# A two-layer encoder on one core: the MLP in two phases through DRAM, with the up product as a chained seven-product block product

## The chip, the core and the metric

The kernel runs on one core of a Trainium2 chip. The metric is the device time of one launch in microseconds. The kernel before takes 1725.45 us (median of three runs, 1725.27 to 1726.40).

## The reference, cut to what matters

Two sequences of 512 and 256 tokens (768 together) with 1024 features pass through two layers of different mixers. Behind each mixer stands the same MLP with 4096 hidden features:

```python
def trunk(x, w):
    for layer in range(DEPTH):                 # two layers
        ...                                    # mix: Hyena and attention, or conformer and pooling
        x = layer_norm(DN_ALPHA * x + mix, w['ln1_g'][layer], w['ln1_b'][layer])
        h = jnp.square(jax.nn.relu(x @ w['mlp_w1'][layer])) @ w['mlp_w2'][layer]
        x = layer_norm(DN_ALPHA * x + h, w['ln2_g'][layer], w['ln2_b'][layer])
    return x
```

All is float32. The kernel gets float32 precision out of TensorE's rounded format (fp32r) by splitting every operand into a high part (a ScalarE copy that rounds) and a low part (a VectorE subtraction of the high part from the source). A product of two split operands is three matmuls, high by high, high by low and low by high.

## The kernel before

The MLP is the function `mlp`, called once per layer. `self.acc[0..5]` holds six token tiles of 128 tokens by 1024 features; `x` holds the same, transposed and split, in `quad` tiles. The 32 tiles of 128 hidden features are taken in eight chunks of four.

**Up.** `feature_tile` makes one hidden tile for 384 tokens: eight contraction steps of three matmuls with 384 columns. A hidden tile needs two such calls, so one layer has 32 x 2 x 8 x 3 = 1536 matmuls of 384 columns. The weights of a tile come by `weights` (load `raw`, copy `wh`, subtraction `wl`). ScalarE applies ReLU (L507) and square (L509) and the tile stays in SBUF as `sq`.

**Down.** The second product of the first seven chunks is a two by two block product in Winograd's form: tokens, hidden tiles and output columns are cut in halves, and seven block products take the place of eight. `operands` makes the left operands of a pair of hidden tiles (four sums of 384 columns on VectorE, L518, then splits). `moving` loads four blocks of weights (`mraw`), makes four sums of them on GpSimd (L518) and splits the seven right operands. A block product is three PSUM banks (`s`, `b`, `o`) by two hidden tiles by three matmuls of 512 columns: 18. Each product is added to the token tiles or to partial sums `u` by VectorE (L569, L594), or from `u` by GpSimd (L569). The last chunk is a plain product, so that the token tiles end one after another and each goes through its layer norm.

**Order.** A generator hands out two products behind each hidden tile, so up and down alternate on TensorE all through the MLP. Loads and weight splits are given high priority and run ahead. Five weight slots in two rings (`self.rings`) hold the split `wh` and `wl`. Each engine works its own instructions in order; SyncE (SP) issues the loads in order, and each load waits there until its buffer is free.

## Time and profile before

| | us |
|---|---|
| median of three runs | 1725.45 |
| span of the profiled execution | 1726.3 |
| TensorE (PE) busy | 1635.3 |
| VectorE (DVE) busy | 1310.8 |
| ScalarE (ACT) busy | 741.0 |
| GpSimd (POOL) busy | 676.7 |

The first MLP lies at about 468 to 945 us of the span, the second at 1212 to 1711 us. The profile lists busy time, waits by releaser, instructions in order of time, and in windows the busy time of every engine with the clock that TensorE was granted (1.00 is its full 2.4 GHz). PE rows show an instruction from its start to its modelled end, and successive matmuls overlap, so their pace is read from start to start.

### The profile page before, as it was taken

What the parts mean: (1) busy time and instruction counts of PE and PEld (TensorE: products, weight loads), DVE (VectorE), ACT (ScalarE), POOL (GpSimd) and SP (SyncE); (2) the same over time, 40 slices, a digit from 0 to 9 for tenths busy, and PEclk for the clock granted to TensorE, in tenths of its full rate; (3) what the DMA queues carried; (4) which work ended last, traced back from release to release, by engine and by line L of the source; (5) the groups of instructions that cost most, each with busy time, mean ns of one, the idle gap of its engine ahead of it and who ended that gap; (6) DMA issues with size and microseconds to landing.
All of it is one profiled execution on the core that took longest, in us unless ns stands there. A gap on an engine that the chain in (4) does not pass through costs nothing.

```text
span 1726.3 us, 21545 instructions
## 1 busy us (share of the span) xinstructions
PE 1635.3 (95%) x8308; PEld 1444.5 (84%) x8308; DVE 1310.8 (76%) x1828; ACT 741.0 (43%) x1115; POOL 676.7 (39%) x423
## 2 busy tenths in 40 slices
PE   8999979999899999999999899687999999999997
PEld 6878767878799999999998788466999999999996
DVE  5786887874777677777776899998677777777767
ACT  5633335662344344344342455445444434434431
POOL 1364552110624325324421489754422532442323
PEclk9999979999999999999999899898999999999999
DMA  6331142023211221221111212122222122112101
GB/s 233 115 110 63 37 141 75 28 96 122 98 61 50 86 69 42 86 86 49 62 62 62 66 52 93 43 74 68 93 84 74 41 82 86 50 62 86 61 26 73
DMA packets 43366, 131.32 MB, mean 76 GB/s; under 512 B 5040, under 2 KB 7544, under 8 KB 43264
## 3 DMA queue, kind: packets, MB, share of 16 engines
q1 hardware_dynamic: 43264, 129.95, 22.8%
q8 instruction: 65, 1.06, 0.3%
q14 instruction: 37, 0.30, 0.1%
HBM read 122.03 MB, written 7.90 MB: 75 GB/s over the span
## 4 chain that ended last, share of the span: by engine, by line
PE 74%; DVE 18%; ACT 3%; issue 2%; DMA 2%; POOL 1%; SPq 0%; DVEq 0%; ACTq 0%; POOLq 0%
PE a L275 11%; PE a L274 11%; PE a L276 11%; PE b L274 5%; PE b L275 5%; PE o L275 4%; PE b L276 4%; PE o L276 4%; PE o L274 4%; PE s L275 4%; PE s L274 4%; PE s L276 4%; DVE co L1276 3%; DVE wl L249 2%; DVE o L1276 2%
## 5 line engine op out<-in xcount | busy, mean ns | idle before, releaser
L274 PE MATMUL a<-quad,wh 128*128 128x384 f32 (+2 forms) x1248 | 411.3, 330 | 2.5 <-ACT quad L241 1.3
L275 PE MATMUL a<-quad,wh 128*128 128x384 f32 (+2 forms) x1248 | 411.7, 330 | 0.4 <-DVE quad L249 0.2
L276 PE MATMUL a<-quad,wl 128*128 128x384 f32 (+2 forms) x1248 | 411.4, 330 | 0.0
L518 POOL TENSOR_TENSOR mraw<-mraw,mraw 128x1024 f32<-128x1024 f32 x56 | 175.3, 3140 | 245.5 <-issue 233.6
L569 POOL TENSOR_TENSOR acc<-acc,u 128x512 f32<-128x512 f32 x84 | 130.7, 1588 | 328.0 <-DVE u L594 328.0
L249 DVE TENSOR_TENSOR wl<-mraw,wh 128x1024 fp32r<-128x1024 f32 x98 | 135.1, 1378 | 143.6 <-ACT wh L241 143.6
L274 PEld LDWEIGHTS a<-quad,wh 128*128 128x128 f32 x1248 | 235.0, 188 | 7.9 <-ACT quad L241 1.8
L275 PEld LDWEIGHTS a<-quad,wh 128*128 128x128 f32 x1248 | 235.3, 189 | 6.2 <-DVE quad L249 1.4
L249 DVE TENSOR_TENSOR wl<-raw,wh 128x1024 fp32r<-128x1024 f32 x112 | 150.0, 1339 | 117.3 <-ACT wh L241 117.1
L276 PEld LDWEIGHTS a<-quad,wl 128*128 128x128 f32 x1248 | 235.4, 189 | 1.5
L241 ACT ACTIVATE wh<-raw 128x1024 fp32r<-128x1024 f32 x127 | 134.0, 1056 | 177.8 <-PE a L275 79.9
L241 ACT ACTIVATE wh<-mraw 128x1024 fp32r<-128x1024 f32 x98 | 104.0, 1061 | 172.5 <-PE a L275 100.9
L507 ACT ACTIVATE sq<-a 128x384 f32<-128x384 f32 x128 | 61.4, 480 | 146.2 <-PE a L276 133.3
L274 PE MATMUL s<-quad,wh 128*128 128x512 f32 (+1 forms) x224 | 87.0, 388 | 10.9 <-ACT quad L241 6.0
L1273 POOL TENSOR_TENSOR c<-c,c 128x512 f32<-128x512 f32 (+1 forms) x63 | 77.0, 1224 | 43.6 <-ACT c L1272 40.3
L569 DVE TENSOR_TENSOR acc<-acc,s 128x512 f32<-128x512 f32 x112 | 73.9, 680 | 24.9 <-ACT u L603 24.9
L569 DVE TENSOR_TENSOR acc<-acc,o 128x512 f32<-128x512 f32 x124 | 82.8, 678 | 9.9 <-PE o L276 9.7
L275 PE MATMUL s<-quad,wh 128*128 128x512 f32 (+1 forms) x224 | 87.0, 388 | 1.4 <-DVE quad L249 1.4
L276 PE MATMUL s<-quad,wl 128*128 128x512 f32 (+1 forms) x224 | 86.5, 386 | 0.0
L569 DVE TENSOR_TENSOR acc<-acc,b 128x512 f32<-128x512 f32 x124 | 82.0, 679 | 1.2 <-PE b L276 1.0
L249 POOL TENSOR_TENSOR wl<-raw,wh 128x1024 fp32r<-128x1024 f32 x15 | 39.2, 2612 | 70.6 <-ACT wh L241 59.5
L1276 DVE SCALAR_TENSOR_TENSOR co<-hp,cols,co 128x256 f32<-128x256 f32 x88 | 66.0, 792 | 0.1
(516 smaller groups left out, 3865.5 us busy)
## 6 DMA issues: line engine op xcount, KB each, us to landing
raw<-in_w SPq DMA_DIRECT2D x72, 512.0 KB
mraw<-in_w SPq DMA_DIRECT2D x56, 512.0 KB
raw<-in_w_hy SPq DMA_DIRECT2D x12, 512.0 KB
raw<-in_w_oi SPq DMA_DIRECT2D x12, 512.0 KB
raw<-in_w_oo SPq DMA_DIRECT2D x12, 512.0 KB
raw<-in_w_eo SPq DMA_DIRECT2D x8, 512.0 KB
raw<-in_w_mla SPq DMA_DIRECT2D x6, 512.0 KB
zy<-in_xT SPq DMA_DIRECT2D x12, 256.0 KB
```

The source lines that it names most:

```text
L241: self.nc.scalar.activation(dst, src, AF.Copy)
L249: e.tensor_tensor(out=dst, in0=src, in1=hi.bitcast(F32), op=ALU.subtract)
L274: mm(out, a[0], b[0], start=start, stop=False)
L275: mm(out, a[0], b[1], start=False, stop=False)
L276: mm(out, a[1], b[0], start=False, stop=stop)
L507: nc.scalar.activation(sq[m][:, off : off + n], ps[:, :n], AF.Relu)
L518: eng.tensor_tensor(out=o, in0=a, in1=b, op=op)
L569: (nc.vector if eng == "dve" else nc.gpsimd).tensor_tensor(out=av, in0=av, in1=v, op=ALU.add)
L1273: nc.gpsimd.tensor_tensor(out=c2, in0=c2, in1=c3, op=ALU.add)
L1276: last = nc.vector.scalar_tensor_tensor(out=v, in0=hp[:, k : k + n], scalar=w(k), in1=v, op0=ALU.mult, op1=ALU.add)
```

## The change

`mlp` is split into `up_phase` and `down_phase`, and the hidden operands go through DRAM between them.

- **Up phase.** Hidden tiles are taken in 16 pairs. The first two pairs are plain, as before (4 x 2 x 8 x 3 = 192 matmuls of 384 columns). For the other 14 the up product is itself a two by two block product (features, hidden tiles and tokens by halves): seven products of 4 x 3 matmuls of 384 columns, 84 for a pair. The three accumulators `c`, `y`, `z` are each one PSUM bank; a later product is chained on an earlier one by accumulating in the same bank, and a copy (`u1`, `u2`, `v7`) is taken in between.
- **Operands of the up phase.** `token_operands` makes four sums of `acc` for each of three token tile pairs, 128 x 512 each (three on GpSimd, nine on VectorE), transposes them (48 transposes of 128 x 128) and splits them. `operands(q)` loads two weight tiles, makes four 512-column sums on GpSimd and cuts 3.5 tiles into high and low parts; before, a pair needed two.
- **Store.** The squares and their sums for the down product (four sums of 384 columns on VectorE per pair, as before) go unsplit to DRAM: `a`, `b`, `s` and `s4`, 1.376 MB for a pair. The last two pairs are stored plain.
- **Down phase.** The 14 pairs come in chunks of 4, 4, 4 and 2 pairs. Each of the seven products reloads its left operand (`hr`, up to 128 x 1536) and splits it (`hh`, `hl`), and is three banks by n pairs by three matmuls of 512 columns. Products are chained in PSUM here too, so a chunk of four pairs needs 15 additions of 512 columns on VectorE and six on GpSimd. Eight sums of 1024 columns on GpSimd make the weights of a chunk (two for each of the four). The last two pairs follow as a plain product with the layer norms.
- The residual factor on `acc` stands between the phases (six GpSimd instructions). The pool of the next layer's `x` is opened after the down phase.

The diff, cut to its core:

```diff
+    def token_operands(self, xt, tmp):
+        for t in range(3):
+            a, b = self.acc[t], self.acc[t + 3]
...
+            for i, p, q, e in (
+                (0, b[:, :512], a[:, :512], nc.vector), (2, b[:, 512:], b[:, :512], nc.gpsimd),
+                (1, b[:, 512:], d[0], nc.vector), (3, a[:, 512:], d[1], nc.vector),
+            ):
+                e.tensor_tensor(out=d[i], in0=p, in1=q, op=sub)
+            for i in (1, 2, 0, 3):
...
+                    nc.tensor.transpose(ps[:, j * P : j * P + P], d[i][:, j * P : j * P + P], self.ident)
+                self.split(*(q[:, :, t * P : t * P + P] for q in T_[i]), src)
...
+            def operands(q):
...
+                    wa = self.cut(ra)
+                    tt(s[:, h0], rb[:, h0], rb[:, h1], add)
+                    tt(s[:, h1], s[:, h0], ra[:, h0], sub)
+                    ws = self.cut(s)
+                    tt(rb[:, h0], ra[:, h0], rb[:, h0], sub)
+                    wb = self.cut(rb)
+                    tt(ra[:, h1], ra[:, h1], s[:, h1], sub)
+                    w4 = self.cut(ra[:, h1], 512)
...
+                product("1", c, True)
+                nc.scalar.activation(u1, c, AF.Copy)
+                product("2", y, True)
+                tt(ha[:, :HT], u1, y, add, nc.vector)
+                product("6", c, False)
+                nc.scalar.activation(u2, c, AF.Copy)
+                product("7", z, True)
+                nc.scalar.activation(v7, z, AF.Copy)
+                product("5", c, False)
+                tt(hb[:, HT:], v7, c, add, nc.vector)
+                product("4", z, False)
+                tt(hb[:, :HT], u2, z, add, nc.vector)
+                product("3", c, False)
...
+                store(q, ha, hb)
...
+            def left(q0, n, i, c):
...
+                    r = self.t(db, [P, 4, HT], "hr", bufs=3)[:, :n]
+                    nc.sync.dma_start(r, src if c is None else src[:, :, c * HT : c * HT + HT])
+                    v = [self.t(db, [P, 4, HT], f"h{g}", F32R, bufs=3)[:, :n] for g in "hl"]
+                    self.split(*v, r)
...
+            for q0, n in CHUNKS:
...
+                product(xb, 0, 0, True)
+                copies(u)
+                out(0, 0, u, nc.gpsimd)
+                product(yb, 1, 0, True)
+                out(0, 0, yb)
+                product(xb, 2, 1, False)
+                copies(u2)
+                out(1, 0, u2, nc.gpsimd)
+                product(yb, 0, 1, True)
+                out(1, 1, yb)
+                product(xb, 2, 0, False)
+                out(1, 1, xb)
+                product(yb, 1, 1, False)
+                out(1, 0, yb)
+                product(xb, 3, None, False)
+                out(0, 1, xb)
...
+        self.up_phase(l, x, hs)
+        xs.close()
+        for t in range(NT):
+            nc.gpsimd.tensor_scalar(out=self.acc[t], in0=self.acc[t], scalar1=ALPHA, scalar2=None, op0=ALU.mult)
+        self.down_phase(l, hs)
```

Where this moves instructions is read from the built programs. First SP, in the middle of the MLP before: loads of both weights follow one another (`in_w1_0` and `in_w2_0` are the weights of the first layer).

```order
L540 DMA mraw_1153_6109<-in_w2_0 128x1024 [waits DMAHW5_49,Pool_49]
L540 DMA mraw_1154_6111<-in_w2_0 128x1024 [waits DMAHW6_49,DVE_49]
L266 DMA raw_1193_6329<-in_w1_0 128x1024 [waits DVE_49]
L540 DMA mraw_1155_6113<-in_w2_0 128x1024 [waits DMAHW0_49,DVE_49]
L540 DMA mraw_1156_6115<-in_w2_0 128x1024 [waits DMAHW1_49,DVE_49]
```

On SP in the kernel after, at the end of the up phase; `hs` and `hp` are the hidden operands in DRAM, `a` and `b` are squares written by ScalarE:

```order
L555 DMA hp1_864_4236<-b_1185_6297 128x768 [waits Activation_49]
L555 DMA hp0_863_4235<-a_1184_6296 128x768 [waits Activation_49]
L555 DMA hp1_866_4238<-b_1204_6427 128x768 [waits DMAHW5_49,DVE_49,Activation_49]
L555 DMA hp0_865_4237<-a_1203_6426 128x768 [waits DMAHW6_49,Activation_49]
L687 DMA hr_1223_6555<-hs0_847_4219 128x4x384 [waits DMAHW7_49,PE_49]
L654 DMA mraw_1226_6561<-in_w2_0 128x1024 [waits DMAHW0_49]
L687 DMA hr_1238_6627<-hs1_848_4220 128x4x384 [waits DMAHW1_49,PE_49]
L654 DMA mraw_1227_6563<-in_w2_0 128x1024 [waits DMAHW2_49,PE_49]
L687 DMA hr_1245_6682<-hs2_849_4221 128x4x384 [waits DMAHW3_49]
L654 DMA mraw_1228_6565<-in_w2_0 128x1024 [waits DMAHW4_49]
```

The first load of the down phase stands behind the store of the last pair; the loads of `in_w2_0` that stood among the loads of `in_w1_0` now all come after it.

Second GpSimd, at a chunk's start. Before, the four weight sums of a chunk stood in one piece ahead of the additions to `acc`:

```order
L518 TENSOR_TENSOR mraw_898_4573<-mraw_899_4575,mraw_898_4573 128x1024 [waits DMAHW1_49,DMAHW0_49,DVE_49]
L518 TENSOR_TENSOR mraw_899_4575<-mraw_900_4577,mraw_899_4575 128x1024 [waits DMAHW2_49,Pool_49]
L518 TENSOR_TENSOR mraw_907_4613<-mraw_900_4577,mraw_898_4573 128x1024
L518 TENSOR_TENSOR mraw_901_4579<-mraw_901_4579,mraw_907_4613 128x1024 [waits DMAHW3_49,DVE_49,Pool_49]
L569 TENSOR_TENSOR acc3_778_3647<-acc3_778_3647,u0_895_4564 128x512 [waits DVE_49]
```

And GpSimd after, at the start of the first chunk of the down phase (`mraw_1248` and `mraw_1249` are the right operand of the third product):

```order
L640 TENSOR_TENSOR mraw_1226_6561<-mraw_1230_6569,mraw_1226_6561 128x1024 [waits DMAHW0_49,DMAHW6_49,DVE_49,Pool_49]
L694 TENSOR_TENSOR acc0_775_3644<-acc0_775_3644,u0_1217_6549 128x512 [waits Activation_49]
L640 TENSOR_TENSOR mraw_1227_6563<-mraw_1231_6571,mraw_1227_6563 128x1024 [waits DMAHW2_49,DMAHW7_49,DVE_49,PE_49]
L694 TENSOR_TENSOR acc1_776_3645<-acc1_776_3645,u1_1218_6550 128x512 [waits Activation_49]
L694 TENSOR_TENSOR acc2_777_3646<-acc2_777_3646,u2_1219_6551 128x512 [waits Activation_49]
L640 TENSOR_TENSOR mraw_1248_6688<-mraw_1232_6573,mraw_1226_6561 128x1024 [waits DMAHW0_49,PE_49,Pool_49]
L640 TENSOR_TENSOR mraw_1230_6569<-mraw_1232_6573,mraw_1230_6569 128x1024
L640 TENSOR_TENSOR mraw_1249_6689<-mraw_1233_6575,mraw_1227_6563 128x1024 [waits DMAHW1_49,Pool_49]
L640 TENSOR_TENSOR mraw_1231_6571<-mraw_1233_6575,mraw_1231_6571 128x1024
```

The sum that the third product needs now stands behind the additions to `acc`, which wait for ScalarE's copies of the first product.

Third ScalarE. Before, the copies of summed weights stood among ReLU, squares and hidden operands:

```order
L241 ACTIVATE wh_1072_5605<-mraw_1068_5597 128x1024 [waits DMAHW5_49,PE_49]
L241 ACTIVATE obh_1009_5233<-sq_1001_5167 128x768 [waits PE_49]
L507 ACTIVATE sq_1042_5431<-a_1043_5432 128x384 [waits DVE_49,PE_49]
L241 ACTIVATE wh_1078_5639<-mraw_1077_5637 128x1024 [waits Pool_49]
L241 ACTIVATE wh_1084_5675<-raw_1083_5673 128x1024 [waits DMAHW3_49,PE_49]
```

After, at the start of the down phase, behind the first splits:

```order
L251 ACTIVATE wh_1243_6639<-mraw_1229_6567 128x1024 [waits DMAHW5_49]
L719 ACTIVATE u0_1217_6549<-s_1211_6543 128x512 [waits PE_49]
L719 ACTIVATE u1_1218_6550<-b_1212_6544 128x512 [waits PE_49]
L719 ACTIVATE u2_1219_6551<-o_1213_6545 128x512 [waits PE_49]
L251 ACTIVATE hh_1255_6744<-hr_1254_6742 128x1536 [waits DMAHW2_49,DVE_49]
L251 ACTIVATE hh_1262_6799<-hr_1261_6797 128x1536 [waits DMAHW3_49,DVE_49,PE_49]
L251 ACTIVATE wh_1250_6692<-mraw_1248_6688 128x1024 [waits Pool_49]
L251 ACTIVATE wh_1252_6696<-mraw_1249_6689 128x1024 [waits Pool_49]
```

The copy `hh_1262`, the left operand of the fifth product, waits for PE (its buffer is that of the second product) and stands ahead of `wh_1250`, which the third product needs.

## Rows read from the trace of the kernel before

**Rows 1.** The page: the span, and busy time of each engine.

```profile
span 1726.3 us, 21545 instructions
...
PE 1635.3 (95%) x8308; PEld 1444.5 (84%) x8308; DVE 1310.8 (76%) x1828; ACT 741.0 (43%) x1115; POOL 676.7 (39%) x423
```

**Rows 2.** Windows: busy us of each engine, granted clock, DMA share, GB/s.

```profile
core 0: us, PE busy (x) PEld busy (x) DVE busy (x) ACT busy (x) POOL busy (x), PEclk, DMA share, GB/s
...
448.00:456.00 8.00, 3.93 (x19) 3.00 (x17) 8.00 (x13) 4.58 (x7) 6.54 (x4) 0.71 0.64 194
460.00:500.00 40.00, 38.26 (x222) 37.14 (x221) 24.65 (x28) 17.20 (x26) 16.02 (x7) 1.00 0.17 62
500.00:560.00 60.00, 60.00 (x309) 55.08 (x309) 45.99 (x58) 26.32 (x36) 17.31 (x9) 1.00 0.22 71
700.00:760.00 60.00, 60.00 (x308) 54.93 (x307) 43.57 (x54) 25.69 (x34) 22.12 (x10) 1.00 0.19 62
```

**Rows 3.** Waits of PE in 470 to 940 us, all of them.

```profile
PE a L274 <- ACT sq L507: 1.2, 1, 1.2
```

**Rows 4.** PE in order of time: start, duration, instruction.

```profile
699.71 0.33 PE L274 MATMUL a<-quad,wh 128*128 128x384 f32 x1
...
704.91 0.39 PE L274 MATMUL s<-wh,obh 128*128 128x512 f32 x1
...
710.84 0.39 PE L276 MATMUL b<-wh,oal 128*128 128x512 f32 x1
```

**Rows 5.** PE in order of time: transposes in the layer norm ahead of the MLP.

```profile
447.42 0.60 PE L410 MATMUL o<-ident,acc 128*128 128x128 f32 x4
447.86 0.60 PE L410 MATMUL b<-ident,acc 128*128 128x128 f32 x4
```

**Rows 6.** Instructions by line, 470 to 940 us: count, busy us, mean ns, idle before.

```profile
L249 DVE TENSOR_TENSOR wl<-mraw,wh 128x1024 fp32r<-128x1024 f32 x49 | 67.7, 1382 | 70.3 <-ACT wh L241 70.3
L569 DVE TENSOR_TENSOR acc<-acc,o 128x512 f32<-128x512 f32 x58 | 38.7, 678 | 5.0 <-PE o L276 4.9
L241 ACT ACTIVATE wh<-raw 128x1024 fp32r<-128x1024 f32 x32 | 33.9, 1059 | 47.5 <-PE a L275 29.5 <-PE o L276 15.4 <-DMA raw<-in_w_oi 2.7
L518 POOL TENSOR_TENSOR mraw<-mraw,mraw 128x1024 f32<-128x1024 f32 x28 | 87.7, 3143 | 121.6 <-issue 116.4 <-DVE wl L249 4.7
L569 POOL TENSOR_TENSOR acc<-acc,u 128x512 f32<-128x512 f32 x42 | 65.4, 1589 | 162.7 <-DVE u L594 162.7
L598 POOL TENSOR_SCALAR acc<-acc 128x1024 f32<-128x1024 f32 x1 | 2.8, 2772 | 0.0
```

**Rows 7.** POOL and DVE in order of time, working together at 476 us.

```profile
475.76 7.74 POOL L518 TENSOR_TENSOR mraw<-mraw,mraw 128x1024 f32<-128x1024 f32 x3 [4.67 <-DVE wl L249]
...
478.62 2.63 DVE L518 TENSOR_TENSOR s<-s,sq 128x384 f32<-128x384 f32 x1
```

**Rows 8.** DVE in order of time at 706 us, where POOL has nothing to do.

```profile
706.08 1.23 DVE L249 TENSOR_TENSOR wl<-mraw,wh 128x1024 fp32r<-128x1024 f32 x1 [3.92 <-ACT wh L241]
707.23 0.68 DVE L569 TENSOR_TENSOR acc<-acc,s 128x512 f32<-128x512 f32 x1
707.82 0.55 DVE L518 TENSOR_TENSOR s<-sq,sq 128x384 f32<-128x384 f32 x1
708.29 0.68 DVE L569 TENSOR_TENSOR acc<-acc,b 128x512 f32<-128x512 f32 x1
```

**Rows 9.** Line L518 by form: count, shortest, median and longest ns, first and last start.

```profile
L518 POOL TENSOR_TENSOR mraw<-mraw,mraw x28: 2399/2712/4817, 475.8 to 871.2; 128x1024 f32<-128x1024 f32 x28
```

**Rows 10.** DMA 456.8 to 466.2 us in 40 slices, and SP's five issues there.

```profile
GB/s 0 0 0 0 157 157 192 331 418 349 401 314 401 418 349 453 366 349 279 314 296 366 384 366 418 436 401 436 401 453 366 471 366 279 174 105 87 52 52 0
...
456.88 0.33 SPq L266 DMA_DIRECT2D raw<-in_w  x1
457.26 1.91 SPq L540 DMA_DIRECT2D mraw<-in_w  x4
```

**Rows 11.** The chain of waits in order of time, a load that was waited for.

```profile
413.09 6.80 DMA raw<-in_w
```

More of the change, by code (lines that the diff above doesn't have):

```diff
@@ L202, in _layout, with __init__ @@
     return {k: np.ascontiguousarray(v) for k, v in out.items()}
+class _Slot(list):
+    def __init__(self, parts, chunk):
+        super().__init__(parts)
+        self.chunk = chunk
 class _Encoder:
@@ L270, in weights, with mm3, mm @@
         return h, l
-    def mm3(self, out, a, b, start, stop):
-        mm = self.nc.tensor.matmul
+    def mm3(self, out, a, b, start, stop, more=False):
+        def mm(*k, **kw):
+            self.nc.tensor.matmul(*k, skip_group_check=more, **kw)
         mm(out, a[0], b[0], start=start, stop=False)
@@ new lines, in down_phase, with tt, raw_tile, moving @@
+    def down_phase(self, l, hs):
+        nc, w2 = self.nc, self.d[f"w2_{l}"]
+        add, sub = ALU.add, ALU.subtract
+        def tt(o, a, b, op, eng=nc.gpsimd):
+            eng.tensor_tensor(out=o, in0=a, in1=b, op=op)
+        with self.pool("db") as db:
+            def raw_tile():
+                return self.t(db, [P, 1024], "mraw", bufs=12)
+            def moving(gs):
+                def load(h, c):
+                    r = []
+                    for g in gs:
+                        with self.tc.high_priority():
+                            v = raw_tile()
+                            nc.sync.dma_start(v, w2[g, h, c])
+                        r.append(v)
+                    return r
+                def cut(vs):
@@ L564, in moving @@
                 yield cut(b21)
                 yield cut(b22)
[L567 to L577 removed]
+            def left(q0, n, i, c):
+                with self.tc.high_priority():
+                    r = self.t(db, [P, 4, HT], "hr", bufs=3)[:, :n]
+                    src = hs[q0].chunk[i]
+                    nc.sync.dma_start(r, src if c is None else src[:, :, c * HT : c * HT + HT])
+                    v = [self.t(db, [P, 4, HT], f"h{g}", F32R, bufs=3)[:, :n] for g in "hl"]
+                    self.split(*v, r)
+                return v
@@ new lines, in into, with product @@
+            def into(t, c, v, eng):
+                av = self.acc[t][:, c * 512 : c * 512 + 512]
+                eng.tensor_tensor(out=av, in0=av, in1=v, op=add)
+            for q0, n in CHUNKS:
+                w = moving(range(q0 // 2, (q0 + n) // 2))
+                xb, yb = ([self.bank2(g) for g in "sbo"] for _ in range(2))
+                u = [self.t(db, [P, 512], f"u{j}", bufs=2) for j in range(3)]
+                u2 = [self.t(db, [P, 512], f"u{j}", bufs=2) for j in range(3)]
+                def product(pss, i, c, start):
+                    a, b = left(q0, n, i, c), next(w)
@@ L631, in mlp @@
-            ops = []
-            for i in (0, 2):
-                ops.append(operands(*up(tiles[0][i : i + 2])))
-            for e in range(NE - 1):
-                down = products(e, ops)
-                ops, hid = [], {}
-                for i, m in enumerate(tiles[e + 1]):
-                    (sq,) = up((m,))
-                    if e == NE - 2:
-                        hid[m] = [q for q in zip(*halves("oa" if i < 2 else "ob", sq))]
-                    elif i % 2:
-                        ops.append(operands(prev, sq))
-                    prev = sq
-                    next(down)
@@ L645, in mlp, with copies @@
-            if xp:
-                xq = self.quads(xp)
-            else:
-                xq = None
-            rows = [raw_tile() for _ in range(2)]
-            for j, v in enumerate(rows):
-                nc.sync.dma_start(v, self.d["rows"][row + j : row + j + 1, :].to_broadcast([P, D]))
-            e = NE - 1
-            ws = [[self.weights(w2[c, 2 * e + j]) for j in range(2)] for c in range(2)]
+                        into(3 * r + j, c, v, eng)
+                def copies(us):
+                    for v, ps in zip(us, xb):
+                        nc.scalar.activation(v, ps, AF.Copy)
```

277 lines of the change are left out of this document (148 added, 129 removed).

## The prediction

> **What bounds the kernel now.** I read the windows first. In the middle of an MLP TensorE is busy for all of 60.00 us at a granted clock of 1.00, VectorE for 44 to 46 us, ScalarE for 26, GpSimd for 17 to 22 [rows 2]. The list of waits then names a single wait of TensorE in 470 us, 1.2 us long [rows 3]. So both MLPs are bound by the number of matmuls, and whatever is taken from that number is time saved, provided that TensorE stays as full as it is. The page says the same of the whole: 1635.3 of 1726.3 us busy [rows 1]. In the order of time I read the pace: 30 matmuls of 384 columns from 699.71 to 704.91 us, 0.1733 us each; 26 of 512 columns from there to 710.84, 0.228 us each [rows 4].
>
> **Matmuls removed and added.** The up product falls from 1536 to 192 + 14 x 84 = 1368 matmuls per layer: 168 x 0.1733 = 29.1 us. The down product keeps its number, 882 in blocks and 144 plain. 48 transposes come in; four stand 0.44 us apart [rows 5], so 48 cost 5.3 us. TensorE's own work falls by 23.8 us per layer, 47.6 us in both. That is what the change can win if nothing waits. The rest of the sum is waits, per layer.
>
> **Head of the up phase.** TensorE has the plain pairs and the transposes to do, 192 x 0.1733 less what stands ahead of the transposes: some 32 us by the order of the program. Meanwhile GpSimd must do in order three sums of 512 columns, the six residual scalings of 2.77 us and the four sums of the first pair [rows 6]. At 1.3 to 1.6 us for 512 columns (1.59 is the mean of the like addition; half of the three sums of 1024 columns in 7.74 us is 1.29) that is 26 to 28 us, to which VectorE's subtractions add by holding it up, and splits follow. I take 3 us of wait more than the 1.7 us that 460 to 500 us show now [rows 2]; ends 0 and 8.
>
> **The up pairs.** TensorE needs 84 x 0.1733 = 14.6 us for a pair. VectorE has 3.5 low parts (1.15 us from start to start for 1024 columns), four sums of 384 columns (0.47) and three additions out of PSUM, 7.3 us [rows 8]; GpSimd four sums, 5.1; ScalarE about 8.7 at 1.06 us for 1024 columns [rows 6]; DMA 2.4 MB, 164 GB/s, where five loads moved at 350 to 450 GB/s [rows 10]. No engine is full. The chain load, cut, sum, cut runs through few buffers (a pair's raw weights reuse those of the pair before, and five split slots serve 3.5 tiles a pair); by these durations I count 2 to 3 us of slack in it. I take 2 us per layer; ends 0 and 8.
>
> **From up to down.** Here is the largest term. SP issues in order, and the first load of the down phase stands behind the store of the last pair's squares. Call the end of the last up matmul E. ReLU and square take 1.3 us (by 1.06 us for 1024 columns), the issue 0.4 [rows 6, 10]; the load of 786 KB can start at E + 1.8. A load took 0.9 us from its issue to its first data, and five loads of 512 KB were done 9 us after the first issue, 1.4 to 1.6 us each [rows 10]. So `hr` lands at E + 5 and the first weights at E + 6.3; ScalarE's two copies (1.6 and 1.06 us) and VectorE's low part follow, and TensorE starts at E + 8.7. It then waits at the second pair of weights and ends the first product at E + 20, the second (36 x 0.228 = 8.2 us) at E + 28.5. The third product needs a difference of weights that stands on GpSimd behind a sum, an addition, a sum and two additions, the last of which waits for the first product's copies: the difference is there at E + 28.7 at 2.4 us a sum, its other half, behind one more sum, at E + 33.5. On ScalarE its copy stands behind `hh_1262`, which waits for the end of the second product and takes 1.6 us. So the third product starts at E + 32.4, waits for its other half until E + 35.8 and ends at E + 42.6; the fourth ends at E + 50.8. These four are 32.9 us of matmuls, so 18 us are lost. GpSimd's sums, though, took 3.14 us on the mean and not 2.4 [rows 6]; at that pace 6 us more are lost. I take 20; ends 14 (data and copies early, nothing held up) and 26. The nearest single row, a load that was waited for, took 6.80 us before its copy could begin [rows 11]; that bounds the first stretch from above with little change. Nothing else can fill this stretch: the transposes and the next mixer depend on the down product. Also, after a gap at 448 us the granted clock fell to 0.71 in that stretch, the lower level of 1.2 GHz for part of it [rows 2]; a few matmuls at half speed are in the upper end.
>
> **Chunks of the down phase.** A chunk of four pairs is 252 x 0.228 = 57.5 us. VectorE has 14 low parts of weights (16 us), those of the hidden operands (12) and 15 additions from PSUM (9), 37 us; GpSimd eight sums and six additions, 8 x 2.4 + 6 x 1.28 = 26.9; ScalarE 29; DMA 9.5 MB, 165 GB/s. Each fits, but the first two are not independent. While GpSimd did three sums in 7.74 us, a sum of 384 columns on VectorE took 2.63 us [rows 7]; without GpSimd such a sum took 0.55 and the next began 0.47 later [rows 8]. GpSimd's sums ranged from 2.40 to 4.82 us [rows 9]. VectorE's additions out of PSUM kept 678 ns on the mean of 58 [rows 6], as they have without GpSimd [rows 8]. So VectorE's work from SBUF alone and GpSimd's share one resource: 27.9 + 26.9 = 54.8 of 57.5 us, where before it was about 40 of 62.5. It just fits; I take 1 us for each full chunk, 3 together, ends 0 and 18. The last chunk, two pairs, has the same reckoning on half the matmuls: 28.7 us against some 36 of the shared resource, part of which runs ahead. I take 4, ends 0 and 10. The plain pairs' operands are reloaded behind the sixth product: 1 us, ends 0 and 2.
>
> The Trainium skill (SBUF — State Buffer, section "Who interferes with whom") states that a VectorE instruction with two SBUF inputs and a GpSimd instruction that reads SBUF exclude each other, the first to start holding the port for its whole length. The trace agrees: 0.55 us became 2.63. By that rule the weight sums should go where VectorE has slack, and the change does the opposite, doubling them in the block products' operands; its price is the third rival below.
>
> **The sum.** Per layer -23.8 + 3 + 2 + 20 + 3 + 4 + 1 = +9.2 us; for two layers +18. The profiled execution's span of 1726.3 us stands 0.85 us above the median of 1725.45; I add the difference to the median: 1743.5 us.
>
> **Rivals.** *Faster: the turn is cheap.* If the third and fourth products are not held by GpSimd and `hh_1262`, only the first load and the second weights cost, 12 us; with 2 us at the head and nothing elsewhere a layer gains 10 us: 1705. For it: all engines but TensorE have slack on the mean, and the order of issue leaves GpSimd just 0.2 us late at the first half. Against it: rows of the order say that they are held, and the copy's wait is for TensorE itself. *No change:* the turn costs 16 us and the rest 8, between both: 1725. *Slower, the down phase bound by the shared port:* if the 54.8 us don't interleave with their dependences, each full chunk takes 6 us more, the last 9; with 24 at the turn, 5 at the head, 2 in the pairs and 1 at the plain products the layer loses 59 - 24 = 35 us: 1795. It decides from the point where VectorE's low parts mean over about 1.9 us in the chunks (now 1.38 [rows 6]). *Much slower, the up pairs starve:* if the slack of the weight chain is gone under the same contention, 4 us of each of 14 pairs are lost, 54 more per layer than I took: about 1850. Against it stand 11.0 us of shared work in 14.6.
>
> **How the numbers follow.** A measurement of this kernel tells 0.2% from no change, 3.5 us. My forecast, 1729 to 1770, gets 0.42; the faster rival with all below 1722 gets 0.27; no change 0.12; the shared port 0.14; starving pairs 0.05. So faster 0.27, same 0.12, slower 0.61. With all low ends a layer gives -23.8 + 14 = -10, 1706; below it lies some 0.1. Above 1785 lies the upper part of the two last rivals, another 0.1. The range is 1706 to 1785.
>
> **What will show it.** In the profile after: TensorE full at a clock of 1.00 inside the up pairs, 14.6 us apart; one gap of about 8 us between the phases with a chain of DMA, ScalarE `hh`, `wh`, VectorE, and further waits of the first chunk on `wh` whose releaser is GpSimd; a granted clock below 1.00 there; chunks of about 58 us. I am wrong if those waits sum to under 10 us per layer, if TensorE waits in most pairs, or if chunks take over 63 us.

## The result and the profile after

The changed kernel takes 1769.26 us (median of four runs, 1766.12 to 1772.45) against 1725.36 for the kernel before beside it: a ratio of 1.0253, 95% interval 1.0238 to 1.0267. It is slower by 44 us, where the forecast was slower by 18; the time lies inside the forecast's range. The page of after, answering [rows 1]:

```profile
span 1767.7 us, 21673 instructions
...
PE 1616.2 (91%) x8068; PEld 1411.0 (80%) x8068; DVE 1397.6 (79%) x1654; ACT 823.8 (47%) x1201; POOL 824.1 (47%) x505
```

TensorE has 240 instructions fewer and is busy for 19 us less, and the span is 41 us longer: 60 us of new idle time. The windows of after, columns as in [rows 2], say where it is not:

```profile
500.00:560.00 60.00, 58.77 (x316) 57.82 (x315) 39.01 (x40) 30.32 (x44) 26.63 (x17) 0.94 0.41 140
680.00:740.00 60.00, 48.34 (x243) 43.90 (x241) 33.03 (x31) 29.54 (x37) 18.03 (x10) 0.91 0.70 251
740.00:800.00 60.00, 54.53 (x227) 44.13 (x228) 55.12 (x33) 27.58 (x27) 44.41 (x16) 0.91 0.46 149
800.00:860.00 60.00, 60.00 (x266) 49.71 (x265) 57.76 (x38) 29.39 (x30) 43.26 (x16) 1.00 0.55 175
920.00:960.00 40.00, 30.28 (x127) 24.18 (x126) 23.04 (x35) 8.35 (x10) 3.23 (x1) 0.87 0.39 131
960.00:1000.00 40.00, 25.50 (x118) 19.84 (x117) 39.48 (x78) 13.77 (x24) 16.91 (x19) 0.78 0.14 44
```

The full chunks (800 to 860 us) keep TensorE at 60.00 of 60, though VectorE is at 57.76. The time goes at two places, 680 to 800 (the turn from up to down) and 920 to 1000 (the end of the down phase, here called the **seam**: from the block products to the plain pairs, their layer norms and the next mixer). TensorE's waits in 709 to 766 us, then in 932 to 996 us (total, times, longest); between the two none is listed:

```profile
PE s L284 <- ACT wh L251: 14.0, 2, 9.6
PE s L284 <- DVE wl L259: 3.2, 3, 2.2
...
PE s L429 <- DVE acc L417: 9.6, 2, 8.0
PE o L284 <- ACT hh L251: 9.6, 1, 9.6
PE a L429 <- POOL acc L415: 3.1, 2, 1.7
```

Stage times (first matmul to first matmul), set against the prediction's terms, in us per layer:

| term | forecast | layer 0 | layer 1 |
|---|---|---|---|
| matmuls | -23.8 | -23.8 | -23.8 |
| up phase, head and pairs | +5 | +5.1 | +9.4 |
| turn | +20 | +22.4 | +24.0 |
| chunks | +7 | 0 | 0 |
| reload and plain pairs (seam) | +1 | +22.3 | +4.5 |
| sum | +9.2 | +26.0 | +14.1 |

The row of matmuls is worked out from counts and paces and not measured. Each other row is what a stage took beyond its matmuls, less what the kernel before took beyond its own; in the kernel before, up and down alternate, and what they took beyond their matmuls together is set against the up phase. With 0.9 us in the mixer between, the sums are 41.0 of the 41.4 us between the spans. The seam of the first layer alone is 21 us over its forecast. It is read from SP's issues (start, how long, what) and from the chain of waits of after:

```profile
933.90 2.06 SPq L276 DMA_DIRECT2D raw<-in_w_oi  x2
936.01 0.90 SPq L764 DMA_DIRECT2D hr<-hp  x2
...
943.09 1.25 SPq L764 DMA_DIRECT2D hr<-hp  x2
```

```profile
936.01 5.20 DMA hr<-hp
941.23 0.85 ACT hh L251
942.12 1.22 PE o L284 x2
...
954.10 0.70 DVE acc L777
```

The last block product ends at 932.5. The reload `hr<-hp` (L764) issues at 936.0, because its buffers lie in the pool `ml`, which opens only when the down phase's pool is closed, and because two weight loads of the next mixer (`in_w_oi`) stand ahead of it on SP. It lands at 941.2, and TensorE has stood for 9.6 us. Two of the four operands come later still (943.09), so TensorE works at several token tiles in turn; the first is added at 954.10, and the layer norms crowd behind: from the last matmul of the MLP to the first of the next mixer 17.0 us pass (978.7 to 995.7), where the kernel before took 5.2 (964.1 to 969.3). Layer 1 has no mixer behind it, and there the same costs 4.5.

### The profile page after: what moved, and what is told of

Same layout as the page of the kernel before. It is cut to its first block, busy times and chain, and to the rows that moved or that the text cites. A ratio compares the mean times of both kernels' runs of the same rounds, so it can differ in the third digit from the quotient of the medians.

```text
span 1767.7 us, 21673 instructions
## 1 busy us (share of the span) xinstructions
PE 1616.2 (91%) x8068; PEld 1411.0 (80%) x8068; DVE 1397.6 (79%) x1654; ACT 823.8 (47%) x1201; POOL 824.1 (47%) x505
## 4 chain that ended last, share of the span: by engine, by line
PE 56%; DVE 20%; issue 9%; POOL 6%; DMA 4%; ACT 4%; SPq 0%; DVEq 0%; POOLq 0%; ACTq 0%
PE b L284 16%; PE s L284 14%; PE o L284 12%; PE a L284 11%; DVE wl L259 3%; DVE co L1392 3%; POOL mraw L539 2%; POOL raw L539 2%; DVE o L1392 2%; DMA raw<-in_w 2%; ACT wh L251 1%; DVE acc L407 1%; DVE st L395 1%; DVE acc L417 1%; DVE hl L259 1%
## 5 line engine op out<-in xcount | busy, mean ns | idle before, releaser
L259 DVE TENSOR_TENSOR wl<-raw,wh 128x512 fp32r<-128x512 f32 (+1 forms) x140 | 173.6, 1241 | 97.1 <-ACT wh L251 96.9
L284 PE MATMUL a<-quad,wh 128*128 128x384 f32 (+2 forms) x1024 | 244.8, 320 | 0.8 <-ACT wh L251 0.5
L284 PE MATMUL s<-quad,wh 128*128 128x512 f32 (+2 forms) x800 | 233.2, 371 | 11.2 <-ACT quad L251 6.1
L251 ACT ACTIVATE wh<-raw 128x1024 fp32r<-128x1024 f32 (+1 forms) x155 | 151.5, 980 | 180.9 <-DMA raw<-in_w 70.3
L284 PEld LDWEIGHTS a<-quad,wh 128*128 128x128 f32 x1024 | 178.8, 189 | 6.5 <-ACT wh L251 0.8
L284 PEld LDWEIGHTS s<-quad,wh 128*128 128x128 f32 x800 | 148.1, 192 | 28.8 <-ACT quad L251 6.1
L284 PE MATMUL a<-quad,wl 128*128 128x384 f32 (+2 forms) x512 | 163.5, 319 | 0.0
L259 DVE TENSOR_TENSOR hl<-hr,hh 128x1536 fp32r<-128x1536 f32 (+1 forms) x64 | 131.0, 2049 | 36.2 <-ACT hh L251 36.2
L284 PE MATMUL s<-quad,wl 128*128 128x512 f32 (+2 forms) x400 | 147.8, 369 | 0.0
L284 PEld LDWEIGHTS a<-quad,wl 128*128 128x128 f32 x512 | 96.9, 189 | 1.6
```

The source lines that it names most:

```text
L251: self.nc.scalar.activation(dst, src, AF.Copy)
L259: e.tensor_tensor(out=dst, in0=src, in1=hi.bitcast(F32), op=ALU.subtract)
L284: self.nc.tensor.matmul(*k, skip_group_check=more, **kw)
```

## The experiments

Times stand beside the kernel before on the same chip (1726 to 1727 us). "After" is the changed kernel.

**The reload on ScalarE's queue.**

```diff
-                        r = self.t(mp, [P, T], "hr", bufs=2)
-                        nc.sync.dma_start(r, w)
+                        r = self.t(mp, [P, T], "hr", bufs=2 * (16 - NW))
+                        nc.scalar.dma_start(r, w)
```

> The reload of the last two pairs' hidden operands is issued from ScalarE's queue instead of SP's, with four buffers instead of two. Nothing else changes. Theory (queue): in the first layer the reload stood on SP behind two loads for the next mixer that waited for VectorE, and its second half behind a third that waited for GpSimd; TensorE lost 9.6 us, then some 5 at half clock, and the layer norms of the six token tiles came in one heap, which cost some 11 us behind the last matmul. All of it goes but 1 to 3 us of landing time: about 1769 - 18 = 1751, 1746 to 1756. The second layer, where no such loads stand ahead, gains 0 to 4 of that. Rival (VectorE bound): the layer norms alone need that time on VectorE whatever the reload does; then only the 9.6 us gap goes and part of it comes back at the end: 1762 to 1768.

Measured 1756.85, ratio 1.0175 (1.0160 to 1.0190): 12 us below after. The gap falls from 9.6 to 3.3 us, and the stretch behind it shrinks too: in the first layer the time from the last block product to the next mixer falls by 9.7 us, not quite half of the seam's 22.3. The edit moves the reload to another queue and also gives its raw tiles four buffers in place of two; which of the two gained how much was not separated.

**The chunk of two pairs first.** `CHUNKS = ((0, 2), (2, 4), (6, 4), (10, 4))`, so that the first product needs half the data.

> The chunks of the down phase come as 2, 4, 4, 4 pairs instead of 4, 4, 4, 2. Theory (the turn is bound by the landing of loads): the first chunk needs half the bytes, so the wait of TensorE at the turn falls from 22 to 24 us per layer to 12 to 15 us; the last chunk of four pairs was without waits wherever it stood. About 1769 - 19 = 1750, 1744 to 1756. Rival (the turn is bound by the order on GpSimd and ScalarE): with half the matmuls per product, the waits for the sums stay nearly as long and the second chunk's loads come under the same queue: 1762 to 1770.

Measured 1765.05, 1.0222 (1.0207 to 1.0237). Half the bytes took only 1 us from the first gap (9.6 to 8.5). So it is not the amount of data that most of the gap waits for.

**No weight sums in the down phase.** They are cut to one column, and the third product takes `b22` in place of its sum; this part of the computation is left out.

```diff
-                            tt(o, a, b, sub)
+                            tt(o[:, :1], a[:, :1], b[:, :1], sub)
```

> In the down phase the weight sums on GpSimd are cut to one column, and the third product takes the unsummed block: the sums are left out of what is computed. Theory (landing): the turn keeps most of its wait, 15 us or more of 22 to 24 per layer, since it waits for loads: 1755 to 1765. Rival (GpSimd's chain, as the prediction had it): the wait falls to the first landing and the second weights, about 12 us per layer: 1745 to 1751. In the full chunks VectorE's low parts fall from 2.0 us on the mean to about 1.4, and TensorE, full there already, gains nothing.

Measured 1749.25, 1.0129 (1.0114 to 1.0144). The first gap stays, all that follows it goes:

```profile
PE s L284 <- ACT wh L251: 9.5, 1, 9.5
PE s L284 <- DVE wl L259: 0.3, 1, 0.3
```

So the turn is two things: 9.6 us until the first data are split, and a chain through GpSimd's sums at the third product.

**The first weights loaded during the up phase.** e2's chunks, and three of the first weight blocks loaded early into free `raw` buffers.

```diff
+                early[h, c] = self.raw(self.rings[-r])
+                nc.sync.dma_start(early[h, c], w2[0, h, c])
```

> As with 2, 4, 4, 4 pairs, and three of the first chunk's four weight blocks are loaded into the raw weight buffers of the up phase, ahead of its last stores. Theory (landing): at the turn only the first hidden operands (393 KB) have to land; the wait falls to 6 to 10 us per layer, some 5 us per layer below the run with the small chunk alone: 1769 - 28 = 1741, 1734 to 1748. Rival (order on the engines): no more than 2 us below the small chunk alone.

Measured 1769.67, 1.0242 (1.0225 to 1.0260): nothing won. The first gap is 7.6 us and now waits for `hh`, the left operand, and the up phase, whose buffers were borrowed, grew from 259.2 to 264.5 us.

**The first chunk's sums on VectorE.**

```diff
-                            tt(o, a, b, sub)
+                            tt(o, a, b, sub, nc.vector if gs[0] == 0 else nc.gpsimd)
```

> The eight weight sums of the first chunk of the down phase go to VectorE; those of the other chunks stay on GpSimd. Theory (GpSimd's chain): the second gap of the turn goes (6.5 us in the first layer, 8.4 in the second) and with it the stretch at half clock behind it, some 5 us; VectorE pays 8 x 1.15 us for the sums, part of which delays splits: 15 to 20 us in both layers, 1749 to 1755. Rival (landing): the sums wait for loads that land late and VectorE, in order, holds back the splits behind them: 1764 to 1772.

Measured 1753.56, 1.0149 (1.0132 to 1.0166), as expected: the waits behind the first gap fall from 7.6 and 8.7 us in the two layers to 3.1 and 2.0. GpSimd's chain was their cause.

**Four buffers for the left operands**, `bufs=4` for `hh` and `hl`, which lets `hh_1262` go ahead.

> The split hidden operands of the down phase get four buffers instead of three, so that ScalarE's copy for the fifth product no longer waits for the second product's end ahead of the copy that the third product needs. Theory of the prediction (this wait holds the third product): 3 to 5 us per layer, 1759 to 1763. Rival (GpSimd's sums come later than this copy anyway): 0 to 1 us per layer, 1767 to 1770.

Measured 1771.60, 1.0253 (1.0237 to 1.0268): no change. The hold on `hh_1262`, a step of the prediction, cost nothing in this kernel, where the sums come late as well.

**TensorE kept busy in the gap**, by 40 matmuls of 512 columns that nothing reads.

> Behind the last up matmul of each layer stand 40 matmuls of 512 columns whose result nobody reads; they fill some 9.1 us of the first gap of the turn. They wait for a small copy of the last product, so that nothing else moves. Theory (clock): the first stretch at half clock behind the gap goes, 4 to 6 us per layer: 1757 to 1762. Rival (the matmuls at half clock wait for loads and splits anyway): within 2 us of 1769.

Measured 1776.41, 1.0281 (1.0264 to 1.0299). Windows of after, then of e7:

```profile
720.00:726.00 6.00, 5.67 (x19) 4.05 (x19) 5.00 (x5) 4.53 (x4) 0.00 (x0) 0.73 1.04 397
...
735.00:750.00 15.00, 8.49 (x26) 6.05 (x25) 10.89 (x7) 4.12 (x5) 15.00 (x7) 0.68 0.64 222
```

```profile
720.00:726.00 6.00, 5.21 (x23) 4.33 (x24) 4.99 (x4) 4.58 (x4) 0.00 (x0) 1.00 1.05 400
...
735.00:750.00 15.00, 4.80 (x16) 3.26 (x16) 14.04 (x7) 4.66 (x5) 15.00 (x5) 0.73 0.57 198
```

The granted clock is 1.00 behind the gap in place of 0.73 (part of that stretch at the lower level, 1.2 GHz), and nothing is won: TensorE comes sooner to the third product and waits longer there, with GpSimd busy all 15.00 us. The half clock cost nothing where the sums were late anyway.

The 7 us by which e7 is slower are for the most part not the work of these matmuls. The edit adds a tile `seed` of 448 bytes per partition, and in the built program `hh`, `hl` and three of the five slots of `wh` and `wl` stand 448 bytes higher for it. In the full chunks, with TensorE full at a clock of 1.00, a matmul then takes 229.2 ns from start to start in place of 226.7; by an estimate, 2.5 ns on some 1026 matmuls in each layer are 5 us. What addresses have to do with it comes below.

**All four (e1, e5, e6, e7).**

> Reload on ScalarE's queue with four buffers, first chunk's sums on VectorE, four buffers for the split hidden operands, and the 40 matmuls that nobody reads in the first gap, all together. If the causes add up: 14 + 18 + 4 + 10 less some overlap, 38 to 44 us below 1769: 1725 to 1731, level with the kernel before. Rival (one cause hides behind another, the loads' landing in the end): 1740 to 1750.

Measured 1748.55, 1.0122 (1.0102 to 1.0143). **Only e1 and e5:**

> Only the two edits that gained alone: the reload of the last pairs on ScalarE's queue with four buffers (13 us alone), and the first chunk's sums on VectorE (17 us alone). Theory (they act in different places, so they add up): 1769 - 30 = 1739, 1736 to 1744, below the run with all four edits (1748.6), whose idle matmuls then cost time. Rival (what the one gives the other takes, as in the run with all four): 1746 to 1752.

Measured 1740.92, 1.0083 (1.0063 to 1.0103). The two gains add (12.4 + 15.7 = 28.1, measured 28.3). The run with all four is 7.6 us slower than this one, but it has `seed` too and the same 229 ns, some 5 us by the estimate above; that the unread matmuls themselves cost anything worth naming is not shown, only that they won nothing.

**All down sums on VectorE**, `nc.vector` for every chunk.

> All weight sums of the down phase go to VectorE, in every chunk; GpSimd keeps its six additions a chunk. Theory (shared port): VectorE's low parts of weights in the chunks fall from 2.0 us on the mean to 1.2 to 1.3, so that VectorE, with 8 x 1.15 us more to do, is busy for less of a chunk than the 56 to 58 of 60 us that it shows now; TensorE was full there, so the time is that of the run with the first chunk's sums alone, within 3 us of 1754. Rival (no shared port, VectorE simply has more to do): low parts stay at 2.0 us, the chunks become longer than 57.1 us and the time rises above 1760.

Measured 1752.26, 1.0153 (1.0136 to 1.0171), as e5. What it shows is the shared resource; VectorE's low parts in 800 to 900 us in after, then in e10 (count, busy us, mean ns):

```profile
L259 DVE TENSOR_TENSOR wl<-mraw,wh 128x1024 fp32r<-128x1024 f32 x26 | 52.0, 2011 | 4.1 <-ACT wh L251 4.1
```

```profile
L259 DVE TENSOR_TENSOR wl<-mraw,wh 128x1024 fp32r<-128x1024 f32 x26 | 36.1, 1387 | 14.4 <-ACT wh L251 14.4
```

2011 ns fall to 1387, the value of [rows 6], once GpSimd has no sums to do; TensorE is full both ways, and no time is won in the chunks.

**The last stores on ScalarE's queue** (e9, and the squares of the last two pairs stored from there), so that no store stands ahead of the down phase's loads on SP.

```diff
-                        nc.sync.dma_start(w, v)
+                        nc.scalar.dma_start(w, v)
```

> As the run with the two edits, and the stores of the last two pairs go out from ScalarE's queue, so that SP's first load of the down phase no longer stands behind them. The prediction put the first load 1.8 us behind the last up matmul for that reason: 1.5 to 2 us less in the first gap per layer, 3 to 4 us below that run. Rival (the gap is set by the landing of several loads at once, or ScalarE loses as much by issuing): no change within 1.5 us.

Measured 1729.30, 1.0016 (1.0006 to 1.0026): 11.6 us below e9, three times what was expected. SP in e9, then in e11; the last up matmul ends at 708.5 and 709.6:

```profile
710.00 0.32 SPq L555 DMA_DIRECT2D hp<-a  x1
710.41 0.58 SPq L687 DMA_DIRECT2D hr<-hs  x1
711.04 0.65 SPq L654 DMA_DIRECT2D mraw<-in_w  x1
```

```profile
698.05 0.58 SPq L687 DMA_DIRECT2D hr<-hs  x1
698.69 0.61 SPq L654 DMA_DIRECT2D mraw<-in_w  x1
700.29 0.53 SPq L687 DMA_DIRECT2D hr<-hs  x1
703.30 0.33 SPq L654 DMA_DIRECT2D mraw<-in_w  x1
```

The first load's buffer is free 12 us before the up phase ends, the others' follow; only the two stores ahead of them, which wait for the last square, held them. The gap falls from 9.6 to 4.4 us in both layers.

**The up phase plain**, with no block product and no token operands; the down phase as in after.

> The up phase alone is undone: all 16 pairs are plain (1536 matmuls of 384 columns per layer, no token operands, no weight sums there), stored and reloaded as in the change; the down phase stays. The computation is the same. By the sum 23.8 us of matmuls per layer come back and the up phase's waits (5 to 9 us per layer) go: 1769 + 47.6 - 14 = 1803, 1795 to 1810. Rival (the up block product gains nothing net, its waits eat it): 1769 to 1780.

Measured 1788.56, 1.0359 (1.0344 to 1.0375). TensorE is full in its up phase, with no weight chain to wait for:

```profile
500.00:560.00 60.00, 60.00 (x348) 60.00 (x347) 16.21 (x23) 21.47 (x30) 0.00 (x0) 1.00 0.41 136
```

The up phase ends 13.4 us later than in after (723.4 against 710.0), and in the second layer 11.0 us later, counted from the odd mixer's start. So the up block product nets 11 to 13 us per layer, about two thirds of the 18.8 that the forecast gave it (23.8 less 5). This and the 5.1 of the table do not contradict each other: the plain up phase takes 6.5 us beyond its matmuls in the first layer, the alternating order of the kernel before some 11, so some 5 us of the up phase's waits in the changed kernel are hidden in the table by what the split into two phases saves.

**The plain pairs' operands reloaded during the last chunk** (e11, and `mraw` moved to a pool `dm` on the other side of SBUF that outlives the down phase; the reload uses its slots).

```diff
+                    r = self.t(dm, [P, 1024], "mraw", bufs=12)[:, :T]
+                    nc.scalar.dma_start(r, w)
+                    v = [self.t(dm, [P, 1024], "mraw", F32R, bufs=12)[:, :T] for g in "hl"]
```

> As the run with the two edits and the stores on ScalarE's queue; and the last two pairs' hidden operands are reloaded and split while the last chunk still runs, in the buffers of the weight blocks, which get a pool of their own. Theory (late first token tile): in the first layer the layer norms could begin on VectorE only some 18 us behind the last block product, against 5 in the kernel before, because the plain product worked on several token tiles at once while operands came in; with the operands there at the start, the gap of 3.3 us, the half-clock stretch and 8 to 12 us of the 20 us behind the last matmul go: 1729 - 13 = 1716, 1712 to 1720, faster than the kernel before. The second layer gains 0 to 2. Rival (VectorE's layer norms bound the seam from wherever they start): the gap goes and the end takes it back: 1725 to 1729.

Measured 1739.86, 1.0074 (1.0060 to 1.0088). The seam is gone: no gap, and 2.1 us from the last hidden matmul to the next mixer in place of 20.5. But the turn's gap is 19.1 us. SP in e13:

```profile
703.17 11.01 SPq L654 DMA_DIRECT2D mraw<-in_w  x10
716.04 3.44 SPq L687 DMA_DIRECT2D hr<-hs  x3
```

In this program ten weight loads stand ahead of the first left operand; the next run, where `mraw` is back in its pool, has the old order again.

**The same with the slots of `hr`, `hh` and `hl`.** Only `hh` and `hl` are in `dm`; `mraw` is back.

```diff
-                    v = [self.t(db, [P, 4, HT], f"h{g}", F32R, bufs=3)[:, :n] for g in "hl"]
+                    v = [self.t(dm, [P, 4, HT], f"h{g}", F32R, bufs=3)[:, :n] for g in "hl"]
```

> The kernel of e13 once more, with the same early reload of the hidden operands of the last two pairs, but they now use the slots of hr (raw), hh and hl (split) instead of slots of mraw, so that only hh and hl stand in the pool that outlives the down phase and mraw stands where it did in e11. On SP's queue the first three hr loads then stand ahead of the mraw loads again, interleaved one by one, as in e11. Theory that e13's seam and e11's turn can be had together (the 14 us that each turn lost in e13 came only from ten mraw loads ahead of the first hr): e11's 1729.3 less the 18.4 us of late first token tile that e13 took away in the first layer = 1711, from 1706 to 1716. Rival that the turn is late whatever the order on the queue, because the split of the first operands must wait for a region that the last up products free: turn gaps stay above 12 us in place of 4.4 in each layer, and the time stays at 1725 to 1740.

Measured 1721.56, 0.9976 (0.9965 to 0.9986). The turn's gap is 4.4 us, and 2.4 us pass from the last hidden matmul to the next mixer, both as the theory has it, and yet the time is 10 us above it. No wait explains that. One product's matmuls in 760 to 900 us in e11, then in e14, with the windows:

```profile
L284 PE MATMUL o<-wh,hh 128*128 128x512 f32 x71 | 27.6, 389 | 0.0
...
800.00:860.00 60.00, 60.00 (x267) 49.67 (x266) 57.38 (x41) 29.10 (x29) 42.67 (x16) 1.00 0.52 170
```

```profile
L284 PE MATMUL o<-wh,hh 128*128 128x512 f32 x66 | 26.2, 396 | 0.0
...
800.00:860.00 60.00, 60.00 (x258) 48.24 (x257) 55.00 (x37) 28.83 (x28) 39.87 (x15) 1.00 0.45 151
```

TensorE is full at clock 1.00 in both, and does 258 matmuls where it did 267. From the start of one to the start of the next it is 234 ns on the mean, not 227. The only operands of TensorE that moved are `hh` and `hl`, the stationary ones: in the built program they begin at byte 192480 of a partition in place of 126336.

**Addresses.** Three kernels that move tiles by a few bytes: a pad of 32 bytes in `dm` and in the pool of the token operands (on e14), and 32 and 64 bytes ahead of the down phase's tiles (on e11).

> e14 with one tile of 32 bytes per partition added in the pool of hh and hl and one in the pool of the token operands t1 to t4, which moves hh and hl and the token operands down by 32 bytes, so that they begin at addresses that 64 divides (192448 and 180160 in place of 192480 and 180192). In e14 a matmul of the down phase took 234 ns from start to start where e11 took 227, and one on token operands 176.5 where one on the quads took 174.2; the operands of the slower ones all began 32 bytes off a multiple of 64. Theory that this offset is the cause: the down phase's matmuls go back to 227 ns (7.6 ns on some 1080 matmuls is 8.2 us per layer), those on token operands to 174.2 (2.3 ns on 672 is 1.5 us per layer), and the time falls by 16 to 21 us, to 1701 to 1706. Rival that the place in the memory (the upper end) is the cause and not the offset: 234 and 176.5 ns stay, and the time stays within 3 us of 1721.6.

> e11 with a tile of 32 bytes per partition ahead of the tiles of the down phase, nothing else: u, hr, hh, hl and mraw stand 32 bytes higher, hh and hl in the same part of the memory as in e11. Theory of the 32-byte offset: the down phase's matmuls take 234 ns from start to start in place of 227 and the time rises by some 16 us, to 1743 to 1747. Rival of the place in the memory: 227 ns stay and the time stays within 3 us of 1729.

> e16 with a tile of 64 bytes in place of 32, the control: if the offset within 64 bytes is what counts, matmuls of 227 ns and the time of e11, 1726 to 1732; if any shift at all disturbs e11, as much as e16 shows.

Measured 1725.28 (0.9996, 0.9985 to 1.0007), 1739.24 (1.0081, 1.0067 to 1.0094) and 1740.10 (1.0084, 1.0070 to 1.0097). All three run the down phase at 233 ns from start to start. e16 shows that the place in the memory is not it, since 32 bytes slow e11 down; e15 and e17 that a multiple of 64 is not enough. The theory that a multiple of 64 is enough fell; the next one was a multiple of 128, which 126336 is.

**A pad of 96 bytes on e14**: `hh` begins at 192384 = 1503 x 128.

```diff
+            nc.vector.memset(self.t(dm, [P, 24], "pad"), 0.0)
```

> e14 with a tile of 96 bytes per partition in the pool of hh and hl, nothing else: they begin at 192384, which 128 divides, as it does the 126336 of e11 (227 ns from matmul to matmul); in e14 to e17 they began 96, 64, 32 and 64 bytes off such an address, and all four showed 233 to 234. Theory that an address off a multiple of 128 bytes under the stationary operand is the cause: 227 ns come back at this place too, 7.4 ns on some 1080 matmuls in each layer is 8 us, and the time falls from 1721.6 to 1703 to 1709. Rival that something else of e11's layout gives its 227 ns (the upper end of the memory, the distance to the moving operand): 234 ns stay, and the time stays at 1718 to 1725.

Measured 1710.91, ratio 0.9910 (0.9894 to 0.9927): 10.7 us for 96 bytes, and 267 matmuls again:

```profile
L284 PE MATMUL o<-wh,hh 128*128 128x512 f32 x70 | 27.2, 389 | 0.0
...
800.00:860.00 60.00, 60.00 (x267) 49.69 (x266) 57.03 (x38) 28.76 (x29) 41.43 (x16) 1.00 0.48 152
```

So the offset moves the time, and not the place in the memory. It does not follow that the stationary operand alone counts. In all these kernels the moving operands `wh` and `wl` begin at a multiple of 128, so that an offset of the one is also a difference between the two, and the expectation's rival of the distance to the moving operand stands. e7 speaks for that rival. Its `hh` and `hl` begin 64 bytes off a multiple of 128, as in e17, but three of the five slots of `wh` and `wl` do so too. The chunks of e17, then of e7:

```profile
800.00:860.00 60.00, 60.00 (x259) 48.09 (x258) 55.22 (x39) 28.43 (x28) 40.21 (x15) 1.00 0.51 169
```

```profile
800.00:860.00 60.00, 60.00 (x263) 49.08 (x262) 56.48 (x37) 29.53 (x30) 39.45 (x16) 1.00 0.51 167
```

e17 shows 233 ns, e7 229. It is plainer in the second mixer of e7, where quads that begin 64 bytes off are the moving operand of matmuls with 512 columns: with weights 64 bytes off as well these take 227 ns, with weights at a multiple of 128 they take 233, and in the kernel before, where quads and weights begin at one, 228. So what counts is the addresses of both operands: both at a multiple of 128 gave 227 ns, and so did both 64 bytes off one in that mixer. How far they must agree, and why, was not tried.

The kernel of e18, the change with the edits of e1, e5, e11 and e14 and the pad, is faster than both, by 16 us than the one before and by 58 than the changed one. All of TensorE's waits in it from 707 to 960 us, turn and seam together, where after had 39.5 in 709 to 996:

```profile
PE s L284 <- ACT wh L251: 4.4, 1, 4.4
PE s L284 <- DVE wl L259: 1.8, 3, 1.2
PE b L284 <- DVE wl L259: 1.5, 1, 1.5
PE o L284 <- DVE acc L694: 0.8, 1, 0.8
PE a L429 <- POOL hp L1369: 0.7, 1, 0.7
PE o L284 <- ACT quad L251: 0.7, 1, 0.7
```

## Why the prediction was half right

**The sign** was right: matmuls go, and more is lost in waits. The 23.8 us per layer stand on counts; e12 shows that 11 to 13 of them are left when the up phase's own waits are paid.

**The reload of the plain pairs is the step that failed.** It was put down as "1 us, ends 0 and 2", and measured 22.3 and 4.5. The prediction took the reload to run behind the sixth product and never asked where its buffers come from nor what stands ahead of it on SP, although it did both for the turn. e1 shows the part of the queue and the raw buffers (12 us of the kernel), e13 and e14 the rest: with buffers that exist before the down phase ends, the late first token tile is gone. In both layers together this term was 25 us too small. The errors of the other terms nearly cancel, which is luck: 14 us too many for the chunks stand against 11 too few at the turn and in the up phase, and so the whole sum missed by 23.

**The turn** was right in size (20; 22.4 and 24.0) and half right in its causes. Its first stretch was forecast at 8.7 us and is 9.6 and 9.5; the chain through GpSimd's sums is shown by e3 and e5. The step on `hh_1262` was wrong, since without it no time came back (e6). So was the price of the store at the head of SP's queue: the prediction gave it 1.8 us, from the last matmul on, and did not see that the loads could have gone 12 us before that (e11: 11.6 us for two layers).

**The clock** in the gap was counted as a possible extra cost; e7 shows that filling the gap brings the full clock and no gain in time.

**The chunks** were forecast at 7 us and cost nothing. The third rival's condition was even met, low parts over 1.9 us (2.02 on the mean of the layer), and TensorE did not wait. The resource is shared, as [rows 7, 8] and e10 show, but the work still fits, and the deciding point was set too low. The Trainium skill (SBUF — State Buffer, "Who interferes with whom") has the two engines exclude each other there. The trace agrees that they hold each other up, 2011 ns against 1387; whether the one is shut out for the other's whole length it does not show. The price stayed on VectorE.

**The up phase** was right against the kernel before in the first layer and 4 us short in the second, and against a plain up phase 5 to 8 us short in both (e12). What the difference between the layers is was not tried. A small part of the phase is an operand's address. The matmuls on token operands (`t1` to `t4`, which begin 32 bytes off a multiple of 64 in both layers) are slower than those on the first layer's quads in after, and not in e15, where they begin at a multiple of 64 (520 to 700 us of after, then of e15; the last number is the mean ns):

```profile
L284 PE MATMUL a<-quad,wh 128*128 128x384 f32 x192 | 50.5, 335 | 0.0
L284 PE MATMUL a<-t1h,wh 128*128 128x384 f32 x48 | 16.3, 339 | 0.0
```

```profile
L284 PE MATMUL a<-t1h,wh 128*128 128x384 f32 x48 | 16.1, 335 | 0.0
```

From start to start that is some 176.6 against 173.0 ns; 3.6 ns on 672 matmuls is 2.4 us per layer. That gain did not reach the time in e15: its up phase waited more elsewhere. It does not explain the second layer: there the quads too begin 32 bytes off a multiple of 64, in the kernel before as well, and take some 177 ns in both kernels, where the first layer's take 174.

## What to carry to other kernels

When a stage boundary is put into a kernel, list for every load behind it which buffer it waits for and what stands ahead of it on its queue; a store that waits for the last result must not stand ahead of loads that could go. A kernel that is bound by TensorE pays for every operand that must be fetched at such a boundary, so the next stage's operands need buffers that exist before the last stage ends. And if matmuls grow uniformly slower with TensorE full at its full clock, compare the addresses of both operands in the built program, with those of a run that was faster, before looking for a wait; and when an edit adds a tile, see which operands it moves before its effect on the time is put down to what the edit was meant to do.

## What the runs showed of the hardware that was not expected

- The addresses of a matmul's two operands set its pace. With the moving operand at a multiple of 128 bytes in its partition, a stationary operand 32, 64 or 96 bytes off one made a matmul of 512 columns take 233 or 234 ns in place of 227, low or high in SBUF (e14 to e17), and 227 came back at a multiple of 128 (e18). With both 64 bytes off it was 227 again in the second mixer of e7. The kernel before pays it too: its product behind the first mixer, with quads 96 bytes off a multiple of 128 as the stationary operand, takes 234 ns a matmul, the one behind the second, with quads at one, 227. Token operands 32 bytes off a multiple of 64 as the moving operand cost 3.6 ns on 384 columns (after, e15). Why was not tried.
- GpSimd's sums slow VectorE's low parts from 1387 to 2011 ns without a wait of TensorE (e10).
- A clock of 0.73 behind a gap, lifted to 1.00, won no time (e7).
